# One packed load for the second norm's rows, and three modulation units summed on another engine

## The chip, the core and the metric

The kernel runs on one core of a Trainium2 chip. The metric is device time in microseconds for one execution, from the runtime's measurement; a profiled execution adds a trace, whose span runs from the first to the last instruction that the profiler recorded.

## What is computed

A transformer-like block on 512 tokens of width 1024, batch 1, all in float32. Cut to what matters here:

```
mod = silu(c) @ ada_w + ada_b                       # (1, 6144): six pieces of 1024
sh1, sc1, g1, sh2, sc2, g2 = split(mod, 6)
h = rmsnorm(x, norm1_g) * (1 + sc1) + sh1
xr, gr, u, v = split(h @ w_in, 4)                   # each 512 wide
y_lru = rg_lru(conv(xr)) * gelu(gr)                 # a scan over the sequence
y_sgu = gelu(u) * spatial_gating(gelu(v))
x = x + g1 * (concat(y_lru, y_sgu) @ w_out)
h = rmsnorm(x, norm2_g) * (1 + sc2) + sh2
x = x + g2 * moe(h)                                 # 32 experts, two per token
out = rmsnorm(x, final_g)
```

`ada_w` is 1024 x 6144 floats (25 MB), `w_in` 1024 x 2048, `w_out` 1024 x 1024, and each expert has three matrices of 2 MB, so the experts' 192 MB are most of what is read.

## The kernel before

**Modulation.** `ada_w` is cut into twelve units of 512 columns (`unit`, line 248 and on), each a 1024 x 512 matrix in two tiles of 1 MB, `self.w[0]` and `self.w[1]` (`Ada.load`). Units 0 to 3 feed the first norm, 4 and 5 the gate g1, 6 to 9 the second norm's shift and scale (6 and 8 the shift, 7 and 9 the scale), 10 and 11 the gate g2. `Ada.mm` (line 199) multiplies on TensorE: eight matmuls, one for each block `k` of 128 rows, with the column `cond[:, k]` spread over 32 columns as the stationary operand. Four of them lie side by side in the array, so that four partial sums come out on 32 rows each; ScalarE copies them to a `t2` tile (lines 209 and 211). `columns` (line 213) adds the four partial sums and turns 512 results into four columns, by matmuls with a matrix `quad` of ones at rows 0, 32, 64 and 96; `row` (line 220) does the same to a row on all partitions. `modulate2` (line 401) takes the columns of units 6 to 9 to `s2c`.

**Rows.** The second norm's gain `norm2_g` and the bias of its modulation (`ada_b[3072:5120]`) are wanted as columns in an order in which column `i` of a group holds every fourth element. Lines 257 to 264 load them with eight transfers of single floats, two rows or four rows each, into rows 40 to 63 of `rows_b`; one transpose (line 491) turns all of `rows_b`, and line 493 copies the 24 columns to `cols_g`.

**Order of the work.** SyncE issues nearly all loads, in program order, by hand throughout: an issue that waits for a free buffer holds all behind it. The 1 MB loads of `ada_w`, `w_in`, `w_out` and the first experts share five buffers (`w8`), given out in the order in which the earlier holders are done. Up to line 505 the order on every engine is written by hand; from there to line 830 a planner orders TensorE, VectorE, ScalarE and GpSimd from the program's order and its own estimate of costs and arrivals; then the order is by hand again to line 867. Each engine runs its list strictly in order.

The front: unit 0 and the first half of the `w_in` block for `xr` are loaded, then the rows of line 262, then units 1 and 2, the second half, unit 3 (lines 255 to 268). TensorE turns the normed `x` (line 383), multiplies unit 0, then runs `proj_step` (line 440) over the eight blocks of 128 rows, with units 1 to 3 between the steps: `unit[1].mm(0)` (line 476) after the first step, `unit[1].mm(1)` (line 478) in the midst of the second. Every float32 weight is split on the way into a high part (ScalarE, line 242) and a low part (VectorE, line 244), and a product takes three matmuls (high by high, low by high, high by low).

The middle: four projections (`v`, `gr`, `u` after `xr`), the recurrence, the gating (lines 657 to 671, for four blocks `c`), then the output projection in two halves: the first for all four token tiles, step by step (lines 709 to 722), the second tile by tile (lines 832 to 849), in which routing is worked in. `unit[8].mm` and `unit[9].mm` stand in the `u` projection (lines 649 and 650), `unit[10].mm` in the output projection (line 716), its `row` in the seventh step. `logit_bias` (line 732) works out the router's bias from the shift and scales the router's weights by the scale on GpSimd.

Then the experts, in blocks of two or four: SyncE streams their weights through a ring of buffers (line 1066), TensorE multiplies (lines 1119 and 1166).

Of the kernel before, what the change touches and what calls it, by code (L numbers as in the profile page):

```python
# [7 lines left out]
F32 = mybir.dt.float32  # L8
# [4 lines left out]
OP = mybir.AluOpType  # L13
AX = mybir.AxisListType

P = 128
# [29 lines left out]
def trunk(ctx, tc, a, out):  # L46
    nc = tc.nc
    sync, act, pool, dve, pe = nc.sync, nc.scalar, nc.gpsimd, nc.vector, nc.tensor
# [8 lines left out]
    fp = front.enter_context(tc.tile_pool(name="fp", bufs=1))  # L57
    mixer = ctx.enter_context(ExitStack())
    fa = mixer.enter_context(tc.tile_pool(name="fa", bufs=1, side="right"))
# [4 lines left out]
    def bank(tag=None, shape=(P, 512), dt=F32):  # L64
        if tag is None:
            tag = ring[turn[0] % 3]
            turn[0] += 1
        return psum.tile(list(shape), dt, name=tag)
# [10 lines left out]
    def t2(shape):  # L79
        return ft.tile(list(shape), F32, name="t2", bufs=6)  # L80
# [13 lines left out]
    def paired(v, n):  # L94

        return v.rearrange("p (k c i) -> p k i c", c=P, i=n)
# [9 lines left out]
    off = {}  # L106
# [15 lines left out]
    rows_b = fa.tile([P, P], F32, name="rows_b")  # L122
# [11 lines left out]
    ident = const.tile([P, P], F32, name="ident")  # L134
# [4 lines left out]
    dve.tensor_scalar(before, jp, 0.0, None, op0=OP.is_gt)  # L139
    ones = fp.tile([P, P], BF, name="ones")  # L140
    dve.memset(ones, 1.0)
    onesf = fa.tile([P, 64], F32, name="onesf")
    dve.memset(onesf, 1.0)
    pidx = fa.tile([P, P], F32, name="pidx")
# [20 lines left out]
    n = 0  # L165
# [3 lines left out]
    quad = fp.tile([P, P], F32, name="quad")  # L169
# [9 lines left out]
    class Ada:  # L179
# [18 lines left out]

        def mm(self, kk=None):
            if kk != 1:  # L200
                self.ps = bank("m")
            for k in range(KD) if kk is None else range(4 * kk, 4 * kk + 4):
                j = k % 4
                pe.matmul(self.ps[32 * j:32 * j + 32], cond[:, k:k + 1].to_broadcast([P, 32]), self.w[k // 4][:, j, :],  # L204
                          start=(k < 4), stop=(k >= 4), tile_position=(0, 32 * j))
            if kk != 0:
                self.m = t2((P, 512))
                if self.by4:
                    act.activation(paired(self.m, 1).rearrange("p k i c -> p (k i) c"), paired(self.ps, 4)[:, 0], AF.Copy)
                else:  # L210
                    act.activation(self.m, self.ps, AF.Copy)

        def columns(self):

            ps = bank("m", (P, 4))
            for q in range(4):
                pe.matmul(ps[:, q:q + 1], self.m[:, q * P:(q + 1) * P], quad[:, 0:1], start=True, stop=True)
            return ps

        def row(self, t):  # L220

            ps = bank("m")
            pe.matmul(ps, quad, self.m, start=True, stop=True)
            dve.tensor_tensor(t, ps, t, op=OP.add)

    class Block:
# [19 lines left out]
    unit = [Ada((256 * q, 1024 + 256 * q)) for q in range(4)]  # L246
# [7 lines left out]

    unit[0].load()
    b_xr.load(0)
    n = 40
    for name, ap in (("g2n", a["norm2_g"][0]), ("ada2", a["ada_b"][0, 3072:5120])):
        ap = ap.rearrange("(k c i) -> i k c", c=P, i=4)
        k = 4 * ap.shape[1]  # L260
        for i in range(4):
            sync.dma_start(rows_b[n + i:n + k:4], ap[i])  # L262
        off[name] = n - 40
        n += k
    unit[1].load()
    unit[2].load()
    b_xr.load(1)
# [42 lines left out]
    g2b = const.tile([P, D], F32, name="g2b")  # L310
# [26 lines left out]
    cond = fp.tile([P, KD], F32, name="cond")  # L337
    act.activation(cond, ident[:, 0:KD], AF.Silu)
    pt = bank("m", (P, KD))
# [13 lines left out]
    cols_g = fp.tile([P, 24], F32, name="cols_g")  # L353
# [4 lines left out]
    def cg(name, k):  # L358
        return cols_g[:, off[name] + k:off[name] + k + 4]
# [41 lines left out]
    def modulate2(u, q):  # L401

        ps = u.columns()
        n, sl = 4 * (q // 2), slice(4 * (q // 2), 4 * (q // 2) + 4)
        if q % 2 == 0:
            dve.tensor_tensor(s2c[:, 1, sl], ps, cg("ada2", n), op=OP.add)
            return
        t = small.tile([P, 4], F32, name="modt4")
        dve.scalar_tensor_tensor(t, ps, 1.0, cg("ada2", 8 + n), op0=OP.add, op1=OP.add)
        dve.tensor_tensor(s2c[:, 0, sl], t, cg("g2n", n), op=OP.mult)  # L410
# [24 lines left out]
    def split_to(n):  # L435
        while done[0] < min(n, len(flat)):
            high_to(done[0] + 1)
            low()

    def proj_step(b, k, ps, cs=range(4)):  # L440
        w, x = b.r[k], (hh[:, k, :], hl[:, k, :])
        for n, (i, j) in enumerate(((0, 0), (1, 0), (0, 1))):
            for c in cs:
                sl = slice(c * P, (c + 1) * P)
                lhs, rhs = (x[j][:, sl], w[i]) if b is b_v else (w[i][:, sl], x[j])
                pe.matmul(ps[c], lhs, rhs, start=(k == 0 and n == 0), stop=(k == KD - 1 and n == 2))  # L446

    def banks4():
        return [bank() for c in range(4)]
# [6 lines left out]
    pt = bank("m", (P, P))  # L456
# [17 lines left out]
    ps = banks4()  # L474
# [15 lines left out]
    pt = bank("m", (P, P))  # L490
    pe.transpose(pt, rows_b, ident)
    dve.tensor_copy(cols_b, pt)
    dve.tensor_copy(cols_g, pt[:, 40:64])
    sw = [t2((P, 4, P)) for i in range(2)]
    for i in range(2):
        act.dma_start(sw[i], a["sgu_w"][0].rearrange("h i j -> i h j")[:, 4 * i:4 * i + 4, :])
# [15 lines left out]
    for hp in range(2):  # L512
        pt = bank("m", (P, 4, P))
# [40 lines left out]
    for k in range(KD):  # L554
# [9 lines left out]
        if k == 4:  # L564
            pt = bank("m", (P, 4, P))
# [4 lines left out]
            for c in range(4):  # L570
                dve.scalar_tensor_tensor(sbb[:, c, :], pt[:, c, :], cb_("lnb", c), sbb[:, c, :], op0=OP.mult,
                                         op1=OP.add)
# [8 lines left out]
    for c in range(4):  # L581
        for i, t in enumerate((ra, ia)):
            ps = bank("m")
# [27 lines left out]
    ps = banks4()  # L611
# [31 lines left out]
    ps = banks4()  # L643
    for k in range(KD):
        proj_step(b_u, k, ps)
        if k % 2 == 1:
            split_to(29 + k)
        if k == 1:
            unit[8].mm()
            unit[9].mm()  # L650
        if k == 4:
            modulate2(unit[7], 1)
        if k == 6:
            modulate2(unit[8], 2)
    split_to(36)
    yy.append([l8(F32R), l8(F32R)])
    for c in range(4):
# [3 lines left out]
        for t in range(NT):  # L661
            for h in range(2):
                hd = 2 * c + h
                pe.matmul(sT[64 * h:64 * h + 64, t, :], vn[:, t, hd * 64:hd * 64 + 64], wT[:, hd, :],
                          start=True, stop=True, tile_position=(0, 64 * h))
# [3 lines left out]
                                 op0=OP.mult, op1=OP.add)  # L669
# [39 lines left out]
    ps = banks4()  # L709
    for k in range(KD):  # L710
        for t in range(NT):
            out_step(0, t, k, ps[t])
        if k % 2 == 1:
            split_to(37 + k)
        if k == 0:
            unit[10].mm()
        if k == 2:
            modulate2(unit[9], 3)
        if k == 5:
            unit[11].mm()  # L720
        if k == 6:
            unit[10].row(g2b[:, 0:512])
    split_to(44)
    for t in range(NT):
        out_add(0, t, ps[t])
# [4 lines left out]
        dve.tensor_copy(brep[kk], rep(sh2[:, 4 * kk:4 * kk + 4], P))  # L730

    def logit_bias():
        ps = bank("m", (P, 40))
        for k in range(KD):
            pe.matmul(ps, brep[k // 4][:, k % 4, :], wr[:, k, :], start=(k == 0), stop=(k == KD - 1))
        dve.tensor_tensor(rb, ps, rb, op=OP.add)
        for k in range(KD):
            pool.tensor_scalar(wr[:, k, :], wr[:, k, :], a2[:, k:k + 1], None, op0=OP.mult)
# [93 lines left out]
    for t in range(NT):  # L832
        ps = bank("h")
# [49 lines left out]
    ps = bank("m", (P, E))  # L883
# [412 lines left out]
    for b in range(NB):  # L1296
        q = b // 2
        n = min(2, NB - 2 * (q + 1))
# [14 lines left out]
        else:  # L1313
            n = max(0, len(fill) - FB - FA)
            comb = block(b, [], fill[:n], fill[n:n + FB], fill[n + FB:])
        if b == NB - 2:
            fg = xT4b[((NB - 1) // 2 + 1) % 2].rearrange("p (h k) s -> p h (k s)", h=2)[:, 0]
            for hf in range(2):
                gain = t2((P, 4, P))
                dve.tensor_copy(gain, rep(ca("fg", 4 * hf, 4), P))  # L1320
                ps = bank("m")
# [28 lines left out]
    ms, base, both, v, r = [fin[:, n_parts - 1 + i] for i in range(5)]  # L1350
# [70 lines left out]
```

## Time and profile before

| | |
|---|---|
| median of 3 runs | 723.99 us |
| lowest and highest | 723.14 and 724.71 us |
| the profiled execution: its own time | 725.12 us |
| the profiled execution: span | 723.3 us |
| TensorE busy | 658.3 us (91%) |
| VectorE busy | 297.0 us (41%) |
| ScalarE busy | 178.1 us (25%) |
| granted TensorE clock, mean | 0.962 of full |
| moved by DMA | 246.28 MB, 340 GB/s over the span |

In the rows, PE is TensorE's matmuls, PEld its weight loads, DVE is VectorE, ACT ScalarE, POOL GpSimd, SP SyncE; SPq is an issue of SyncE's DMA queue. Lnnn is a line of the kernel. `out<-in` gives tiles by their names in the program, without numbers; the tiles of the five load buffers are `w`, the PSUM banks are `m`, `h`, `y` and `c`. Times are microseconds from the span's start. A float32 matmul is two records in the trace, so one unit's eight matmuls are `x16`. The clock is the share of full speed that TensorE was granted: 0.50 is 1.2 GHz, 1.00 is 2.4 GHz.

### The profile page before, as it was taken

What the parts mean: (1) busy time and instruction counts of PE and PEld (TensorE: products, weight loads), DVE (VectorE), ACT (ScalarE), POOL (GpSimd) and SP (SyncE); (2) the same over time, 40 slices, a digit from 0 to 9 for tenths busy, and PEclk for the clock granted to TensorE, in tenths of its full rate; (3) what the DMA queues carried; (4) which work ended last, traced back from release to release, by engine and by line L of the source; (5) the groups of instructions that cost most, each with busy time, mean ns of one, the idle gap of its engine ahead of it and who ended that gap; (6) DMA issues with size and microseconds to landing.
All of it is one profiled execution on the core that took longest, in us unless ns stands there. A gap on an engine that the chain in (4) does not pass through costs nothing.

```text
span 723.3 us, 9703 instructions
## 1 busy us (share of the span) xinstructions
PE 658.3 (91%) x3693; PEld 358.2 (50%) x3693; DVE 297.0 (41%) x684; ACT 178.1 (25%) x317; POOL 25.0 (3%) x55
## 2 busy tenths in 40 slices
PE   7699999999998889987999999978799999998773
PEld 6356766777787444432444454513244445442132
DVE  7258638635468843321323333312132333224025
ACT  5135277532255121100101111000010111100114
POOL 3000001000103000000000000000000000000011
PEclk9799999999999999999999999989999999999887
DMA  8699902895528569999999999999999999999993
GB/s 295 200 346 305 318 24 97 271 367 183 218 124 316 218 255 427 400 422 420 421 423 420 420 419 422 420 421 419 423 421 420 420 422 420 421 421 421 383 335 120
DMA packets 68827, 246.28 MB, mean 340 GB/s; under 512 B 11064, under 2 KB 29096, under 8 KB 45224
## 3 DMA queue, kind: packets, MB, share of 16 engines
q1 hardware_dynamic: 67496, 245.08, 86.2%
q8 instruction: 30, 0.49, 0.3%
q10 hardware_dynamic: 1056, 0.52, 0.3%
q14 instruction: 21, 0.17, 0.1%
q0 software_dynamic: 224, 0.02, 0.0%
HBM read 243.51 MB, written 2.10 MB: 340 GB/s over the span
## 4 chain that ended last, share of the span: by engine, by line
PE 64%; DMA 21%; DVE 5%; ACT 4%; SPq 4%; issue 1%; POOL 0%; DVEq 0%; ACTq 0%
PE h L1119 21%; PE y L1166 11%; DMA w8r<-in_expert_w 10%; PE m L955 6%; DMA w<-in_expert_w 5%; PE c L969 4%; DMA l<-in_expert_w 4%; PE c L446 4%; PE h L446 3%; PE m L204 3%; PE y L446 2%; SPq L262 2%; DMA w<-in_ada_w 2%; SPq L1072 1%; PE h L90 1%
## 5 line engine op out<-in xcount | busy, mean ns | idle before, releaser
L1119 PE MATMUL h<-w,l 128*64 128x512 f32 (+1 forms) x616 | 152.5, 615 | 11.0 <-DMA w<-in_expert_w 11.0
L1119 PEld LDWEIGHTS h<-w,l 128*64 128x64 f32 (+1 forms) x616 | 42.8, 128 | 99.3 <-issue 76.6
L970 DVE TENSOR_TENSOR x<-x,c 128x512 f32<-128x512 f32 x96 | 65.8, 685 | 39.0 <-PE c L969 39.0
L1119 PE MATMUL h<-w8r,l 128*32 128x512 f32 (+1 forms) x304 | 69.8, 612 | 2.8 <-DMA w8r<-in_expert_w 2.8
L969 PE MATMUL c<-l,cT 128*128 128x512 f32 x192 | 62.6, 407 | 0.0
L1166 PE MATMUL y<-w8q,gT 128*64 128x512 f32 (+2 forms) x240 | 55.1, 626 | 5.2 <-DMA w8q<-in_expert_w 4.5
L1166 PE MATMUL y<-w8r,gT 128*64 128x512 f32 (+2 forms) x240 | 54.1, 611 | 5.5 <-DMA w8r<-in_expert_w 5.5
L955 PE MATMUL m<-l,b16h 128*128 128x256 f32 (+1 forms) x192 | 51.8, 294 | 3.1 <-ACT l L826 3.0
L994 DVE TENSOR_TENSOR t<-y,g2b 128x512 f32<-128x512 f32 x24 | 16.6, 691 | 92.3 <-PE y L1166 92.3
L1119 PE MATMUL h<-l,l 128*64 128x512 f32 (+1 forms) x120 | 52.5, 609 | 1.5 <-DMA l<-in_expert_w 1.5
L86 ACT ACTIVATE l<-t 128x512 fp32r<-128x512 f32 (+1 forms) x35 | 21.3, 612 | 128.5 <-DVE t L994 118.3
L1146 DVE SCALAR_TENSOR_TENSOR t<-t,ws,h 128x512 f32<-128x512 f32 x13 | 9.7, 747 | 97.2 <-PE h L1119 97.2
L955 PE MATMUL m<-l,b16l 128*128 128x256 f32 (+1 forms) x192 | 49.3, 281 | 0.0
L826 ACT ACTIVATE l<-m,s2c 128x256 f32<-128x256 f32 (+1 forms) x24 | 13.1, 546 | 146.2 <-PE m L955 146.2
L955 PEld LDWEIGHTS m<-l,b16h 128*128 128x128 f32 x192 | 36.3, 189 | 19.7 <-ACT l L826 8.3
L244 DVE TENSOR_TENSOR w8r<-w,w8r 128x512 fp32r<-128x512 f32 x48 | 30.6, 683 | 34.1 <-ACT w8r L242 34.1
L955 PEld LDWEIGHTS m<-l,b16l 128*128 128x128 f32 x192 | 36.3, 189 | 2.4
L1166 PEld LDWEIGHTS y<-w8r,gT 128*64 128x64 f32 (+1 forms) x240 | 15.4, 132 | 42.2 <-issue 30.0
L446 PE MATMUL c<-b16h,w8r 128*128 128x512 f32 x80 | 32.3, 427 | 4.2 <-ACT b16h L415 3.7
L242 ACT ACTIVATE w8r<-w 128x512 fp32r<-128x512 f32 x48 | 26.9, 621 | 33.1 <-PE h L92 14.1
L1119 PEld LDWEIGHTS h<-w8r,l 128*32 128x32 f32 (+1 forms) x304 | 17.8, 123 | 34.3 <-issue 28.9
L969 PEld LDWEIGHTS c<-l,cT 128*128 128x128 f32 x192 | 29.4, 189 | 6.7 <-DVE x L970 4.2
(359 smaller groups left out, 941.3 us busy)
## 6 DMA issues: line engine op xcount, KB each, us to landing
w<-in_expert_w SPq DMA_DIRECT2D x77, 1024.0 KB
w8r<-in_expert_w SPq DMA_DIRECT2D x60, 1024.0 KB
w8q<-in_expert_w SPq DMA_DIRECT2D x30, 1024.0 KB
l<-in_expert_w SPq DMA_DIRECT2D x17, 1024.0 KB
w<-in_ada_w SPq DMA_DIRECT2D x16, 1024.0 KB
w<-in_ada_w SPq DMA_DIRECT2D x16, 512.0 KB
w<-in_w_in SPq DMA_DIRECT2D x8, 1024.0 KB
w<-in_w_out SPq DMA_DIRECT2D x4, 1024.0 KB
```

The costliest lines, as they stand in the source:

```text
L86: act.activation(hi, src, AF.Copy)
L204: pe.matmul(self.ps[32 * j:32 * j + 32], cond[:, k:k + 1].to_broadcast([P, 32]), self.w[k // 4][:, j, :], start=(k < 4), stop=(k >= 4), ti ...
L242: act.activation(hi, raw, AF.Copy)
L244: return lambda: dve.tensor_tensor(lo, raw, hi.bitcast(F32), op=OP.subtract)
L262: sync.dma_start(rows_b[n + i:n + k:4], ap[i])
L446: pe.matmul(ps[c], lhs, rhs, start=(k == 0 and n == 0), stop=(k == KD - 1 and n == 2))
L955: pe.matmul(hold[k], src[:, t, chunk(k)], g[:, t, :], start=(t == 0 and i == 0), stop=(t == NT - 1 and i == 1))
L969: pe.matmul(ps, cT[:, t, :], y[:, cs], start=(i == 0), stop=(i == 1))
L970: dve.tensor_tensor(x2[:, t, cs], x2[:, t, cs], ps, op=OP.add)
L994: dve.tensor_tensor(yf, y, g2b[:, cs], op=OP.mult)
L1119: pe.matmul(h[c:c + n], xT[:, k, c:c + n], w[j][k], start=(k == 0), stop=(k == KD - 1), tile_position=(0, c))
L1166: pe.matmul(y[c:c + n], gT[:, q, c:c + n], w, start=(q == 0), stop=(q == FC - 1), tile_position=(0, c))
```

## The change

The second norm's rows are loaded into a tile of their own, `rows_d`, as six rows of 512 contiguous floats, in two transfers (two rows and four rows) at the same place in SyncE's queue. Four transposes with a step of four elements bring them into the same 24 columns of `cols_g`.

Units 8, 9 and 10 have a new method, `add`, in place of `mm`: for each block `k`, VectorE multiplies the 128 x 512 block of weights by the column `cond[:, k]` and adds it to a `t2` tile, in place. The tile then holds a partial sum on every partition, and `columns` and `row` use a column of ones, `one`, in place of `quad`. The tile keeps the weights' order of columns, so `columns` reads it with a step of four. Unit 8's sums stand in the steps of the `u` projection, those of units 9 and 10 in the steps of the output projection's first half; unit 8's columns move from step 6 of the `u` projection to step 1 of the output projection, unit 9's from step 2 to behind the loop, unit 10's row into `logit_bias`.

```diff
@@ -139,6 +139,8 @@
     dve.tensor_scalar(before, jp, 0.0, None, op0=OP.is_gt)
     ones = fp.tile([P, P], BF, name="ones")
     dve.memset(ones, 1.0)
+    one = fp.tile([P, 1], F32, name="one")
+    dve.memset(one, 1.0)
     onesf = fa.tile([P, 64], F32, name="onesf")
     dve.memset(onesf, 1.0)
     pidx = fa.tile([P, P], F32, name="pidx")
@@ -198,7 +200,7 @@
 
         def mm(self, kk=None):
             if kk != 1:
-                self.ps = bank("m")
+                self.ps, self.sum = bank("m"), quad
             for k in range(KD) if kk is None else range(4 * kk, 4 * kk + 4):
                 j = k % 4
                 pe.matmul(self.ps[32 * j:32 * j + 32], cond[:, k:k + 1].to_broadcast([P, 32]), self.w[k // 4][:, j, :],
@@ -210,17 +212,29 @@
                 else:
                     act.activation(self.m, self.ps, AF.Copy)
 
+        def add(self, k):
+
+            w = self.w[k // 4][:, k % 4, :]
+            if k == 0:
+                self.m, self.sum = t2((P, 512)), one
+                dve.tensor_scalar(self.m, w, cond[:, 0:1], None, op0=OP.mult)
+            else:
+                dve.scalar_tensor_tensor(self.m, w, cond[:, k:k + 1], self.m, op0=OP.mult, op1=OP.add)
+
         def columns(self):
 
             ps = bank("m", (P, 4))
             for q in range(4):
-                pe.matmul(ps[:, q:q + 1], self.m[:, q * P:(q + 1) * P], quad[:, 0:1], start=True, stop=True)
+                m = self.m[:, q * P:(q + 1) * P]
+                if self.sum is one and self.by4:
+                    m = paired(self.m, 4)[:, 0, q]
+                pe.matmul(ps[:, q:q + 1], m, self.sum[:, 0:1], start=True, stop=True)
             return ps
 
         def row(self, t):
 
             ps = bank("m")
-            pe.matmul(ps, quad, self.m, start=True, stop=True)
+            pe.matmul(ps, self.sum[:, 0:1].to_broadcast([P, P]) if self.sum is one else quad, self.m, start=True, stop=True)
             dve.tensor_tensor(t, ps, t, op=OP.add)
 
     class Block:
@@ -254,14 +268,10 @@
 
     unit[0].load()
     b_xr.load(0)
-    n = 40
-    for name, ap in (("g2n", a["norm2_g"][0]), ("ada2", a["ada_b"][0, 3072:5120])):
-        ap = ap.rearrange("(k c i) -> i k c", c=P, i=4)
-        k = 4 * ap.shape[1]
-        for i in range(4):
-            sync.dma_start(rows_b[n + i:n + k:4], ap[i])
-        off[name] = n - 40
-        n += k
+    rows_d = fa.tile([6, 512], F32, name="rows_d")
+    sync.dma_start(rows_d[0:2], a["norm2_g"][0].rearrange("(k f) -> k f", f=512))
+    sync.dma_start(rows_d[2:6], a["ada_b"][0, 3072:5120].rearrange("(k f) -> k f", f=512))
+    off["g2n"], off["ada2"] = 0, 8
     unit[1].load()
     unit[2].load()
     b_xr.load(1)
@@ -490,7 +500,10 @@
     pt = bank("m", (P, P))
     pe.transpose(pt, rows_b, ident)
     dve.tensor_copy(cols_b, pt)
-    dve.tensor_copy(cols_g, pt[:, 40:64])
+    pt = bank("m", (P, 4, 6))
+    for i in range(4):
+        pe.transpose(pt[:, i, :], rows_d.rearrange("r (c i) -> r i c", i=4)[:, i, :], ident[0:6, 0:6])
+    dve.tensor_copy(cols_g.rearrange("p (r i) -> p i r", i=4), pt)
     sw = [t2((P, 4, P)) for i in range(2)]
     for i in range(2):
         act.dma_start(sw[i], a["sgu_w"][0].rearrange("h i j -> i h j")[:, 4 * i:4 * i + 4, :])
@@ -645,13 +658,9 @@
         proj_step(b_u, k, ps)
         if k % 2 == 1:
             split_to(29 + k)
-        if k == 1:
-            unit[8].mm()
-            unit[9].mm()
+        unit[8].add(k)
         if k == 4:
             modulate2(unit[7], 1)
-        if k == 6:
-            modulate2(unit[8], 2)
     split_to(36)
     yy.append([l8(F32R), l8(F32R)])
     for c in range(4):
@@ -712,14 +721,13 @@
             out_step(0, t, k, ps[t])
         if k % 2 == 1:
             split_to(37 + k)
-        if k == 0:
-            unit[10].mm()
-        if k == 2:
-            modulate2(unit[9], 3)
+        unit[9].add(k)
+        unit[10].add(k)
+        if k == 1:
+            modulate2(unit[8], 2)
         if k == 5:
             unit[11].mm()
-        if k == 6:
-            unit[10].row(g2b[:, 0:512])
+    modulate2(unit[9], 3)
     split_to(44)
     for t in range(NT):
         out_add(0, t, ps[t])
@@ -730,6 +738,7 @@
         dve.tensor_copy(brep[kk], rep(sh2[:, 4 * kk:4 * kk + 4], P))
 
     def logit_bias():
+        unit[10].row(g2b[:, 0:512])
         ps = bank("m", (P, 40))
         for k in range(KD):
             pe.matmul(ps, brep[k // 4][:, k % 4, :], wr[:, k, :], start=(k == 0), stop=(k == KD - 1))
```

## Rows read from the trace of the kernel before

**Rows 1.** The profile page: the chain that ended last, by engine.

```profile
PE 64%; DMA 21%; DVE 5%; ACT 4%; SPq 4%; issue 1%; POOL 0%; DVEq 0%; ACTq 0%
```

**Rows 2.** From 270 us: TensorE's wait (total, times, longest); two windows, GB/s last.

```profile
PE h L1119 <- DMA w<-in_expert_w: 11.0, 8, 2.3
...
262.00:271.00 9.00, 8.29 (x42) 3.51 (x44) 0.76 (x2) 0.60 (x1) 0.00 (x0) 1.00 0.26 83
271.00:290.00 19.00, 18.82 (x98) 8.80 (x96) 7.03 (x13) 3.02 (x5) 0.00 (x0) 1.00 1.01 424
```

**Rows 3.** SyncE's queue, 0 to 60 us: start, duration, issue (x: how many merged).

```profile
9.51 10.19 SPq L262 DMA_DIRECT2D rows_b<-in_norm_g  x4
19.73 4.06 SPq L262 DMA_DIRECT2D rows_b<-in_ada_b  x4
23.84 9.21 SPq L194 DMA_DIRECT2D w<-in_ada_w  x8
```

**Rows 4.** Windows of the front: length, busy PE PEld DVE ACT POOL, clock, DMA share, GB/s.

```profile
16.00:17.00 1.00, 0.55 (x8) 0.00 (x0) 0.00 (x0) 0.38 (x1) 0.00 (x0) 1.00 0.95 346
17.00:18.00 1.00, 0.73 (x7) 0.73 (x7) 0.00 (x0) 0.70 (x2) 0.00 (x0) 1.00 0.35 54
...
24.00:25.00 1.00, 1.00 (x4) 0.81 (x3) 0.00 (x0) 0.00 (x0) 0.00 (x0) 0.50 0.28 2
...
26.00:27.00 1.00, 0.19 (x1) 0.00 (x0) 0.00 (x0) 0.00 (x0) 0.00 (x0) 0.87 0.96 314
...
30.00:31.00 1.00, 1.00 (x8) 0.00 (x0) 0.00 (x0) 0.00 (x0) 0.00 (x0) 0.50 1.00 343
```

**Rows 5.** Timeline of the front: ScalarE and TensorE, with idle time before and its releaser.

```profile
18.80 1.15 ACT L242 ACTIVATE w8r<-w 128x512 fp32r<-128x512 f32 x2 [1.09 <-DMA w<-in_w_in]
...
25.56 0.63 PE L446 MATMUL c<-b16l,w8r 128*128 128x512 f32 x1
29.65 1.94 PE L204 MATMUL m<-w,cond 128*32 128x512 f32 x8 [3.46 <-DMA w<-in_ada_w]
...
34.34 1.06 PE L204 MATMUL m<-w,cond 128*32 128x512 f32 x8 [0.46 <-DMA w<-in_ada_w]
35.33 0.50 PE L446 MATMUL y<-b16h,w8r 128*128 128x512 f32 x1
...
36.83 0.95 PE L217 MATMUL m<-quad,t 128*128 128x1 f32 x8
...
41.54 2.78 PE L204 MATMUL m<-w,cond 128*32 128x512 f32 x16
```

**Rows 6.** What TensorE waited for, 36 to 118 us (first) and 118 to 190 (second).

```profile
PE c L446 <- DVE w8r L244: 0.5, 1, 0.5
...
PE m L204 <- DMA w<-in_ada_w: 1.0, 1, 1.0
```

**Rows 7.** Timeline of TensorE: unit 8's matmuls and the next one.

```profile
135.86 1.92 PE L204 MATMUL m<-w,cond 128*32 128x512 f32 x16
137.71 0.50 PE L446 MATMUL c<-b16h,w8r 128*128 128x512 f32 x1
```

**Rows 8.** Windows of the middle, columns as in rows 4.

```profile
150.00:158.00 8.00, 8.00 (x51) 5.46 (x44) 0.48 (x3) 0.66 (x2) 0.00 (x0) 1.00 1.05 387
158.00:170.00 12.00, 11.98 (x105) 8.09 (x104) 10.04 (x16) 7.17 (x13) 0.00 (x0) 1.00 0.50 169
170.00:182.00 12.00, 12.00 (x58) 10.06 (x57) 2.83 (x6) 2.31 (x4) 0.00 (x0) 1.00 0.70 264
```

**Rows 9.** The convolution's lines 548 and 550: duration in ns, least, median, most.

```profile
L548 DVE TENSOR_SCALAR l<-l,cols_b x4: 537/538/546, 66.2 to 74.2; 128x512 f32<-128x512 f32 x4
...
L550 DVE SCALAR_TENSOR_TENSOR l<-l,cols_b,l x12: 739/742/750, 67.2 to 77.9; 128x511 f32<-128x511 f32 x4, 128x510 f32<-128x510 f32 x4, 128x509 f32<-128x509 f32 x4
```

**Rows 10.** SyncE's issue of w_out's last blocks; the output projection's second half, first matmul.

```profile
166.88 1.23 SPq L234 DMA_DIRECT2D w<-in_w_out  x2
...
190.74 0.39 PE L90 MATMUL h<-w8r,l 128*128 128x512 f32 x1
```

## Prediction

> **What bounds the kernel now.** I read the page's chain of waits first [rows 1]. TensorE holds 64% of the chain, DMA 21%. The DMA part lies late: from 270 us on TensorE waits 11.0 us for one kind of the experts' buffers alone, while before 271 the transfers wait for TensorE: between 262 and 271 us they moved 83 GB/s, then 424 [rows 2]. So the expert stream is full from 271 us to near the end, its length is fixed by its bytes, and it starts when TensorE frees buffers. Whatever brings TensorE to 271 us sooner brings the end sooner by as much.
>
> Then the front. SyncE's queue needs from 9.5 to 23.8 us to issue the eight small transfers of line 262, and only behind them stands unit 1's load [rows 3]. The windows show what this does: the transfer engines move 346 GB/s until 17, and from 18 to 25 next to nothing (2 GB/s), with about a quarter of the engines' time still busy [rows 4]. TensorE's list answers: the first projection's last matmul starts at 25.56; unit 1's halves start at 29.65 and 34.34, both when their data lands [rows 5]. That is a stall on the chain.
>
> Last the stretch 118 to 190 us: TensorE waited there 1.0 us in all, so it is the bound [rows 6], and three modulation units of 1.85 us each [rows 7] are what the change takes away. VectorE beside it is idle for long: 0.48 busy of 8 us in 150 to 158, 10.04 of 12 in 158 to 170, 2.83 of 12 in 170 to 182 [rows 8].
>
> **Front: the rows.** Removed are eight transfers in 4-byte elements (24 x 128 of them); added are two with 2 KB rows, at the same place in the queue. Two issues, even at the 1.0 us of each of the later four (4.06 for 4), end by 11.5, so unit 1's load follows there instead of at 23.84 [rows 3]. The stream then does not dry up at 17.5; unit 1's 2.1 MB at 346 GB/s take 6.1 us, so they land by about 24 to 25. The projection ends at 25.56 + 0.43 = 26.0. Unit 1's first half is there, and what is late next is TensorE itself.
>
> How fast it goes from there depends on its clock. The granted clock was 0.50 from 20 to 25, 0.87 in 26 to 27 (so it rose to 2.4 GHz about 0.26 us into that stretch, after five microseconds of matmuls), stayed 1.00 while the engine idled, and was back at 0.50 (1.2 GHz) in 30 to 31 [rows 4]. I take it that without the idle stretch it stays up: the half unit costs 0.26 us slow and 0.86 x 0.99 = 0.85 fast (0.99 is 34.34 to 35.33), together 1.1; the six matmuls behind it 1.5 (35.33 to 36.83) [rows 5]. The second half starts at 26.0 + 1.1 + 1.5 = 28.6 instead of 34.34: 5.7 us gained. If the clock fell anyway, the half costs the 1.9 of the one at 29.65 and the six 6 x 0.43 = 2.6 (0.43 is 512 columns at 1.2 GHz): start at 30.5, 3.8 gained. The Trainium skill, "TensorE: Matmul & The Clock Gate", Part 1, holds that the slow clock is the default, that activity lifts it and idleness brings it back; by that the sum is the first one, and this trace agrees, since the clock came up after the matmuls and fell after the wait.
>
> One cost: the first block of w_in, which line 242 awaits at 18.80 [rows 5], has unit 1's stream behind it now. Between 17 and 18 only 0.35 of the engines' time was busy [rows 4]; if the late engines had to share with full ones it would land at most 0.65 us later, at least 0. I take 0.3, near the middle. The front's gain is 5.4, between 3.2 and 5.7.
>
> The rest of this edit is nothing. Four more transposes of six rows stand ahead of the fifth projection step: about 4 x 0.12 us, by the eight one-column matmuls of line 217 in 0.95 [rows 5]. TensorE waits there 0.5 us for a split of VectorE anyway [rows 6]; if that cover is gone, 0.5 us. The copy of the 24 columns and the memset are one short VectorE instruction each.
>
> **Middle: units 8, 9 and 10.** TensorE loses three times eight packed matmuls; one unit holds it 135.86 to 137.71 = 1.85 us [rows 7], three 5.6, or 5.8 by the 1.92 that the row itself gives. ScalarE loses three copies. The column sums and unit 10's row remain, the row moved in front of the router bias: same TensorE time, and its VectorE addition falls where VectorE waits for that bias.
>
> Added on VectorE: per unit one scaling and seven multiply-adds, each reading its predecessor's result. The nearest rows are the causal convolution's, the same two forms over the same width, in place: 0.54 + 7 x 0.74 = 5.7 us a unit [rows 9], 17.2 in all. Unit 8's fall into the idle time before 158. Units 9 and 10 have 11.4 us to find, and 7.5 us idle in 150 to 158, 2.0 in 158 to 170 and 9.2 in 170 to 182 [rows 8]. If unit 9's go early and all of unit 10's land among the spatial-gating work, that work ends 5.7 - 2.0 = 3.7 us later, and at worst the output projection waits as long; at best nothing waits. I take 0.2, near nothing, since the later projection steps that need those results are the fifth and on: four steps of twelve matmuls, some 3 us each by the six in 1.5, lie between.
>
> What stands behind these instructions: VectorE's queue is in order, and behind a sum that waits for its weights stand the low halves of w_out's splits and the gating products, for which TensorE waits. And the sums free the load buffers later than the matmuls did, which holds SyncE's queue: unit 8's frees the second block of w_out, unit 10's now frees w_out's last two blocks (issued 166.88) and the first expert loads. Those blocks are first multiplied at 190.74 [rows 10], over 20 us later, so this costs nothing until unit 10 is some 15 us late.
>
> The middle's gain: 5.6 - 0.2 = 5.4, between 5.6 - 3.7 = 1.9 and 5.8.
>
> **Sum.** 5.4 + 5.4 = 10.8. The profiled execution took 725.12 us, 1.8 beyond its span; it becomes 714.3. It lies 1.1 above the median of the runs, 723.99, which becomes 713.2. Bounds: least gain 3.2 + 1.9 = 5.1, 718.9. Most: 5.7 + 5.8, plus 0.9 if the slow stretch at 41.54 (a whole unit in 2.78 instead of 1.85, [rows 5, 7]) doesn't come back, plus the 1.0 of waiting in the middle [rows 6]: 13.4, 710.6.
>
> **Rivals.**
> - *Front only.* VectorE's sums delay gating or splits by as much as TensorE saves. For it: VectorE is 10.04 of 12 us full where the gating runs. Against: the idle stretches on both sides. 723.99 - 5.4 = 718.6. Chance 0.12.
> - *Middle only.* Unit 1 would not come sooner, because the new transfers, too, take long or the queue was full anyway. For it: one issue of line 262 sat until the stream had passed. Against: from 18 to 25 there was no stream to be full of. 723.99 - 5.4 = 718.6. Chance 0.05.
> - *Neither*: both of these, or the gain lost on the way to 271 us. 724. Chance 0.04.
> - *Slower.* Unit 10's sums come last in VectorE's queue, its buffers come free late, SyncE's queue holds w_out's last blocks, and TensorE stands before the second half of the output projection. It decides from the point where unit 10's first half is freed after about 185 us of the old time (190.74 [rows 10], less some 5 for a block: 3.0 to load 1 MB at 346 GB/s [rows 4], 1.15 for a split [rows 5], and an issue), and each further microsecond costs one; to pass 725.4 it must eat 10.8 + 1.4 = 12.2, so free it at 197. VectorE's work up to 182 plus 11.4 fits long before. 727 for a release near 199. Chance 0.04.
>
> **How the numbers follow.** The forecast, both gains within their bounds, has 0.75: 713.2. The range 710.6 to 718.7 takes in the bounds of both and the one-sided rivals at 718.6, and leaves out some 0.1. About 0.2% (1.4 us) is what a measurement of this kernel can tell from no change. Faster by more: 0.75 + 0.12 + 0.05 = 0.92; within: 0.04; slower: 0.04.
>
> **What would show it.** Right: line 262 gone, unit 1's load issued near 10, the stream above 300 GB/s through 17 to 25, line 204's third and fourth half units near 26.0 and 28.6 with the clock up; the output projection's second half starting near 180 instead of 190.7; the expert stream full from about 260. Wrong in the front: a wait for unit 1 still there, or the clock down between 27 and 31. Wrong in the middle: TensorE waiting for VectorE (splits, gating or a sum) between 118 and 190, by more than the 1.0 of before. Wrong as a whole: both stages shorter but the expert stream not starting sooner.

## The result, and the profile after

The changed kernel takes **713.85 us** (median of 4 runs, 712.62 to 714.13) where the kernel before, run beside it, takes 724.35 (723.14 to 725.71): a ratio of 0.9848, 95% interval 0.9827 to 0.9868. The profiled execution took 712.62 us with a span of 710.8, 12.5 less than before, at a mean granted clock of 0.983 against 0.962.

The front first. SyncE's queue from 9 to 30 us (start, duration, issue), which answers to [rows 3]:

```profile
10.43 1.15 SPq L272 DMA_DIRECT2D rows_d<-in_norm_g  x1
11.62 0.27 SPq L273 DMA_DIRECT2D rows_d<-in_ada_b  x1
11.94 12.31 SPq L196 DMA_DIRECT2D w<-in_ada_w  x8
```

Unit 1's load now follows at 11.94 instead of 23.84. The windows of the changed kernel (length, busy PE PEld DVE ACT POOL, clock, DMA share, GB/s; [rows 4] before) show that the stream no longer dries up:

```profile
17.00:18.00 1.00, 0.29 (x5) 0.01 (x1) 0.00 (x0) 0.66 (x2) 0.00 (x0) 1.00 1.08 365
...
20.00:21.00 1.00, 0.26 (x1) 0.26 (x2) 1.00 (x3) 1.00 (x2) 0.00 (x0) 1.00 1.11 356
...
24.00:25.00 1.00, 1.00 (x4) 0.63 (x2) 0.00 (x0) 0.00 (x0) 0.00 (x0) 0.50 1.10 347
25.00:26.00 1.00, 1.00 (x10) 0.16 (x8) 0.00 (x0) 0.00 (x0) 0.00 (x0) 0.94 1.10 346
...
30.00:31.00 1.00, 1.00 (x10) 0.92 (x8) 0.83 (x2) 0.66 (x2) 0.00 (x0) 1.00 1.06 382
```

From 24 to 25 us 347 GB/s were moved where it had been 2, and from 26 to 31 TensorE is busy throughout at a granted clock of 1.00 (2.4 GHz). Its timeline over the same stretch ([rows 5] before):

```profile
24.82 0.54 PE L456 MATMUL c<-b16l,w8r 128*128 128x512 f32 x1
25.29 1.07 PE L206 MATMUL m<-w,cond 128*32 128x512 f32 x8
...
27.89 1.06 PE L206 MATMUL m<-w,cond 128*32 128x512 f32 x8
...
34.60 1.92 PE L206 MATMUL m<-w,cond 128*32 128x512 f32 x16
```

Both halves of unit 1 run without a wait, the second at 27.89 instead of 34.34. Unit 2 starts 6.9 us sooner (34.60 for 41.54) and takes 1.92 instead of 2.78, so in this execution the slow stretch there is gone.

In the middle, first the waits of TensorE from 112 to 190 us (total, times, longest; [rows 6] before). Then the weight loads of the column sums in line 231 (LDWEIGHTS; duration in ns: least, median, most; first and last start), with `quad` and with `one`. Then one group of column sums on the timeline:

```profile
PE m L206 <- DMA w<-in_ada_w: 0.9, 1, 0.9
PE m L744 <- DVE t L738: 0.4, 1, 0.4
```

```profile
L231 PEld LDWEIGHTS m<-quad,t x48: 186/192/192, 18.0 to 136.4; 128*128 128x128 f32 x48
...
L231 PEld LDWEIGHTS m<-one,t x16: 308/329/332, 154.5 to 176.7; 128*128 128x128 f32 x16
```

```profile
175.31 1.80 PE L231 MATMUL m<-one,t 128*128 128x1 f32 x8
```

Here is something that was not in the forecast. The column sums of units 8 and 9, which now read their weights in place with a step of four floats, take 1.80 us a group where the others take 0.95 [rows 5], because each weight load takes 329 ns instead of 192. There is also a new wait of 0.4 us ahead of the router bias.

VectorE in the same kernel (the sums are lines 220 and 222; in square brackets the idle time before, and what ended it):

```profile
131.44 3.90 DVE L222 SCALAR_TENSOR_TENSOR t<-w,cond,t 128x512 f32<-128x512 f32 x5
...
159.69 6.71 DVE L222 SCALAR_TENSOR_TENSOR t<-w,cond,t 128x512 f32<-128x512 f32 x10
173.47 0.69 DVE L697 TENSOR_TENSOR t<-h,g1b 128x512 f32<-128x512 f32 x1 [7.07 <-PE h L92]
```

After the last sum VectorE idles 7.07 us, so the sums have room. SyncE's last loads of `w_out`, which unit 10's buffers could have held up, go out from 161.13 on, against 166.88 [rows 10]:

```profile
161.13 5.01 SPq L248 DMA_DIRECT2D w<-in_w_out  x2
```

Counted from the first scan, which is itself 8.1 us sooner, that is 2.3 us later, but TensorE does not wait for them. The output projection's second half starts at 176.97, where the forecast said near 180.

At the end, two windows 12 us earlier than those of [rows 2], and from the list of TensorE's waits, from 258 us on, the one shown there:

```profile
250.00:259.00 9.00, 7.95 (x42) 4.04 (x44) 0.65 (x2) 0.60 (x1) 0.00 (x0) 1.00 0.28 88
259.00:278.00 19.00, 18.80 (x98) 9.26 (x96) 7.14 (x13) 3.02 (x5) 0.00 (x0) 1.00 1.01 423
```

```profile
PE h L1128 <- DMA w<-in_expert_w: 11.9, 9, 1.5
```

The expert stream is full from 259 instead of 271 and as full as before (423 GB/s for 424); what the earlier stages save arrives at the end.

Four landmarks of TensorE and VectorE make the ledger: the first scan of the recurrence, the first matmul of the router bias, the first expert matmul, and the span's end (723.3 before, 710.8 after). Before:

```profile
120.27 1.21 DVE L608 TENSOR_TENSOR_SCAN l<-l,l 128x512 f32<-128x512 f32 x1
...
195.69 1.87 PE L735 MATMUL m<-wr,t 128*128 128x40 f32 x16
...
242.41 7.51 PE L1119 MATMUL h<-w,l 128*64 128x512 f32 x33
```

After:

```profile
112.19 1.22 DVE L621 TENSOR_TENSOR_SCAN l<-l,l 128x512 f32<-128x512 f32 x1
...
183.99 1.95 PE L744 MATMUL m<-wr,t 128*128 128x40 f32 x16 [0.45 <-DVE t L738]
...
230.41 7.51 PE L1128 MATMUL h<-w,l 128*64 128x512 f32 x33
```

So the part up to the scans is 8.1 us shorter, scans to bias 3.6 (75.4 to 71.8), bias to experts 0.3, experts 0.5.

### The profile page after: what moved, and what is told of

The parts are those of the page before. It is cut to its first block, busy times and chain, and to the rows that moved or that the text cites. A ratio compares the mean times of both kernels' runs of the same rounds, so it can differ in the third digit from the quotient of the medians.

```text
span 710.8 us, 9636 instructions
## 1 busy us (share of the span) xinstructions
PE 644.6 (91%) x3649; PEld 358.5 (50%) x3649; DVE 312.3 (44%) x709; ACT 176.3 (25%) x314; POOL 25.0 (4%) x55
## 4 chain that ended last, share of the span: by engine, by line
PE 33%; DMA 28%; SPq 1%; DVE 1%; ACT 1%; issue 0%; ACTq 0%
PE h L1128 15%; DMA w<-in_expert_w 11%; DMA w8r<-in_expert_w 10%; PE y L1175 8%; DMA l<-in_expert_w 7%; PE m L964 4%; PE c L978 4%; SPq L1081 1%; PE m L1143 1%; PE m L986 1%; ACT l L835 0%; PE m L992 0%; DVE x L1370 0%; DVE x L1391 0%; ACT x L1390 0%
## 5 line engine op out<-in xcount | busy, mean ns | idle before, releaser
L1128 PE MATMUL h<-w,l 128*64 128x512 f32 (+1 forms) x616 | 148.4, 601 | 12.0 <-DMA w<-in_expert_w 11.9
L1128 PE MATMUL h<-w8r,l 128*32 128x512 f32 (+1 forms) x304 | 70.9, 607 | 4.3 <-DMA w8r<-in_expert_w 4.3
L1175 PE MATMUL y<-w8r,gT 128*64 128x512 f32 (+2 forms) x240 | 51.7, 590 | 7.4 <-DMA w8r<-in_expert_w 7.4
L1175 PE MATMUL y<-w8q,gT 128*64 128x512 f32 (+2 forms) x240 | 52.2, 592 | 5.5 <-DMA w8q<-in_expert_w 4.5
L1128 PE MATMUL h<-l,l 128*64 128x512 f32 (+1 forms) x120 | 50.8, 593 | 1.6 <-DMA l<-in_expert_w 1.6
L456 PE MATMUL c<-b16h,w8r 128*128 128x512 f32 x80 | 30.8, 411 | 3.0 <-ACT b16h L425 3.0
L1146 DVE SCALAR_TENSOR_TENSOR ws<-m,of 128x4 f32<-128x4 f32 (+1 forms) x13 | 2.1, 163 | 70.4 <-PE m L1143 70.4
```

The lines of the kernel that those rows point to most:

```text
L1128: pe.matmul(h[c:c + n], xT[:, k, c:c + n], w[j][k], start=(k == 0), stop=(k == KD - 1), tile_position=(0, c))
L1175: pe.matmul(y[c:c + n], gT[:, q, c:c + n], w, start=(q == 0), stop=(q == FC - 1), tile_position=(0, c))
```

## The experiments

No kernel here leaves out part of the computation; one adds matmuls whose result nobody reads. Each time is a median of several runs, beside runs of the kernel before in the same series (723.59, 723.82 and 723.64 us in the three series). The intervals are 95% intervals of the ratio to the kernel before.

### The two halves alone

Edits: the kernel before with the hunks on `rows_d` and its four transposes only (first), and with the hunks on `one`, `Ada.add`, `columns`, `row` and their calls only (second).

> The kernel before with the two packed row transfers alone. Theory (the two edits gain separately, the rows 8.1 us by the traces of before and after at 105 us): unit 1's second half on TensorE near 28, clock up at unit 2's matmuls, 8.1 us less than before, some 716. Rival (unit 1's wait gives only the 5.4 us of the forecast, the rest comes from the units): some 718.5.

> The kernel before with the three units' sums on VectorE alone; the eight transfers in single floats stay. Theory (the units gain 4.0 us by the traces): some 720, TensorE's front as before. Rival (the sums fit only because the front had drawn everything ahead): no gain, 724. Rival (they gain the 5.4 forecast): 718.6.

Rows only: **719.51 us**, ratio 0.9941 (0.9924 to 0.9959), 4.1 us gained. Units only: **720.08 us**, 0.9949 (0.9931 to 0.9967), 3.5 gained. By the landmarks the halves lie where they should: scans to bias take 75.3 us with the rows alone, as before, and 71.8 with the units alone, as after. So 3.6 us is what the units' edit is worth there. The rows' gain is less sharp: 4.1 us by the medians, 6.7 by the first scan of the two profiles (113.6 for 120.3). TensorE's timeline of the rows-only kernel shows one reason:

```profile
27.79 1.06 PE L204 MATMUL m<-w,cond 128*32 128x512 f32 x8
...
34.74 3.30 PE L204 MATMUL m<-w,cond 128*32 128x512 f32 x16
```

Unit 1's second half is where the changed kernel has it (27.89), but unit 2 ran at the slow clock, 3.30 us for 1.92. Which matmuls of the front meet the slow clock differs between executions, so one profiled pair cannot give the front's gain to a microsecond.

### Is it the transfers' form or their place?

The kernel before with its eight transfers of single floats, only moved behind unit 3's load (their transpose moved later too); and the changed kernel with the two transfers cut into eight, of 512 bytes a row:

```
     b_xr.load(0)
+    unit[1].load()
+    unit[2].load()
+    b_xr.load(1)
+    unit[3].load()
     n = 40
...
-    unit[1].load()
-    unit[2].load()
-    b_xr.load(1)
-    unit[3].load()
...
```

> The kernel before with its eight transfers in single floats moved behind unit 3's load, and the transpose that needs them behind unit 3's columns. Theory (they hurt only by what stands behind them in SyncE's queue): units 1 to 3 come early, and the transfers fall where the queue has time to spare; most of the 8.1 us kept, 716 to 718. Rival (3072 transfers of 4 bytes slow whatever runs beside or behind them, wherever they stand): the next loads, the v projection's, come late instead, 720 to 724.

```
...
+    for q in range(4):
+        cq = slice(128 * q, 128 * q + 128)
+        sync.dma_start(rows_d[0:2, cq], a["norm2_g"][0].rearrange("(k f) -> k f", f=512)[:, cq])
...
```

> The changed kernel with its two row transfers cut into eight, of 512 contiguous bytes a row. Theory (the elements cost, not the number of issues): each issue some 0.3 to 1 us, unit 1's load issued by 16 at the latest, before the stream runs dry at 17.5; as the changed kernel, 713.8. Rival (eight issues are enough to hold the queue): unit 1 issued near 20 or later, up to 5 us slower.

Moved: **718.15 us**, 0.9926 (0.9901 to 0.995), 5.7 gained, no less than the rows edit. SyncE's queue in that kernel:

```profile
10.49 14.55 SPq L194 DMA_DIRECT2D w<-in_ada_w  x8
...
33.33 7.50 SPq L266 DMA_DIRECT2D rows_b<-in_norm_g  x4
40.87 6.06 SPq L266 DMA_DIRECT2D rows_b<-in_ada_b  x4
```

The single floats hold the queue 13.6 us here (7.50 + 6.06), about as long as in [rows 3], but nothing urgent stands behind them. The price was the place in the queue. Eight issues: **715.18 us**, 0.9879 (0.9844 to 0.9914); its queue, and TensorE's second half of unit 1:

```profile
13.17 5.91 SPq L277 DMA_DIRECT2D rows_d<-in_ada_b  x4
19.12 8.91 SPq L196 DMA_DIRECT2D w<-in_ada_w  x8
```

```profile
29.35 1.06 PE L206 MATMUL m<-w,cond 128*32 128x512 f32 x8 [1.46 <-DMA w<-in_ada_w]
```

Eight issues of longer runs still hold unit 1's load until 19.12, and TensorE waits 1.46 us. Expected was 16 at the latest, and near 20 by the rival, so the issue time is closer to the rival's. The wait is the right size for the 1 us or so by which it is slower than the changed kernel's 713.85 and 714.30 of other series, though the intervals overlap.

### Is the front's gain the clock?

The kernel before with twenty short matmuls put where TensorE waits for unit 1:

```
+    keep_warm(20)
     unit[1].mm(0)
```

> The kernel before with twenty more warming matmuls on TensorE while it waits for unit 1; their result is used nowhere. Theory (the wait also cost clock, which accounts for the part of the front beyond the forecast): the clock stays up, unit 1's second half still starts at 34.3 on its data, but unit 2's matmuls take 1.85 instead of 2.78 us and all behind comes some 1.3 us sooner, 723. Rival (the slow stretch at 40 to 43 us comes from the short waits at 38 to 39): still there, 724.3.

**724.54 us**, ratio 1.0022 (1.0001 to 1.0042). Windows of this kernel, columns as above:

```profile
27.00:28.00 1.00, 1.00 (x11) 1.00 (x11) 0.00 (x0) 0.00 (x0) 0.00 (x0) 1.00 1.08 380
...
30.00:31.00 1.00, 0.94 (x8) 0.19 (x8) 0.00 (x0) 0.00 (x0) 0.00 (x0) 1.00 1.09 363
```

The clock is 1.00 in 30 to 31, where it was 0.50 before [rows 4], and by the medians no time is gained. Unit 2 and the first scan in the same trace:

```profile
40.10 1.92 PE L204 MATMUL m<-w,cond 128*32 128x512 f32 x16
```

```profile
117.60 1.21 DVE L609 TENSOR_TENSOR_SCAN l<-l,l 128x512 f32<-128x512 f32 x1
```

Unit 2 runs fast, as the theory had it and the rival had not, and the first scan and the first expert matmul (239.7) stand 2.7 us sooner than in the profile before. But the experts' stretch took 482.8 us in this execution, for 480.9, and the median is the rival's. The two profiles of the units alone, which have the old front, put the first scan at 118.1 and 119.3, within 2 us of this one; every kernel here with unit 1's load ahead of the small transfers, or behind two packed ones, has it between 111.9 and 114.3. So the front's gain is mainly the data that comes sooner; a gain from the clock alone is not shown by the runs.

### The column sums in order

The changed kernel, with all eight adds of units 8 and 9 writing their sum in the order in which the columns are read, so that the column sums load contiguous weights; and the same with unit 11 on VectorE too:

```
...
+            if self.by4:
+                w = w.rearrange("p (c i) -> p c i", i=4)
+                m = m.rearrange("p (i c) -> p c i", c=P)
...
-            if self.sum is one and self.by4:
-                m = paired(self.m, 4)[:, 0, q]
...
```

> The changed kernel, with VectorE writing units 8 and 9 in the order of the columns, so that the column matmuls read their weights without a step. Theory (the stepped weight load, 329 instead of 192 ns, is what the middle lost): each group of column sums back from 1.66 to about 0.8 us, 1.7 us less than the changed kernel, some 712. Rivals: the sums on VectorE become as much slower by the stepped writing (the same time on the chain if they stay hidden, more if not); or the wait before the router bias takes up what is saved, 713.8.

```
-        if k == 5:
-            unit[11].mm()
+        unit[11].add(k)
```

> The kernel of the run before this one, with unit 11 summed on VectorE as well. Theory (TensorE bounds the output projection, VectorE is idle from 166 to 173 us): 2.0 us less again, some 710. Rival (VectorE is full by then: the sums delay the low halves of w_out's second half and the residual additions): no gain or some us more, 712 to 716.

In order: **711.81 us**, 0.9824 (0.98 to 0.9849). With unit 11 as well: **715.67 us**, 0.989 (0.9847 to 0.9934). The records of the adds (line 227) and of the weight loads (line 234) in the first of them:

```profile
L227 DVE SCALAR_TENSOR_TENSOR t<-w,cond,t x21: 739/1147/1203, 131.3 to 170.9; 128x512 f32<-128x512 f32 x21
```

```profile
L234 PEld LDWEIGHTS m<-one,t x16: 187/192/192, 156.9 to 177.5; 128*128 128x128 f32 x16
```

TensorE's loads are back at 192 ns, but VectorE's adds now pay: 1147 ns in the median where the plain ones take some 750. Of the 1.7 us saved, only 0.6 is seen from scans to bias (71.2 for 71.8), because TensorE now waits 0.7 us for a low half of `w_out`. With unit 11 on VectorE too, that wait (TensorE's waits from 112 to 232 us) becomes

```profile
PE h L92 <- DVE w8r L261: 3.4, 2, 3.1
```

and the stretch from the scans to the experts grows from 117.7 to 122.4 us, so VectorE is the bound there: with the adds of units 8 and 9 as slow as these a fourth unit doesn't fit beside the three. A fourth unit beside plain adds was not run.

### Only the last sum in order, and the parts side by side

Once more the changed kernel and its two halves, in one series, and the changed kernel with only the eighth add of units 8 and 9 in order:

```
...
+                if self.by4 and k == KD - 1:
+                    self.m = t2((P, 512))
+                    out = self.m.rearrange("p (i c) -> p c i", c=P)
+                    m = m.rearrange("p (c i) -> p c i", i=4)
+                    w = w.rearrange("p (c i) -> p c i", i=4)
+                dve.scalar_tensor_tensor(out, w, cond[:, k:k + 1], m, op0=OP.mult, op1=OP.add)
...
```

> The changed kernel as it is, beside its two halves in the same call. If the two halves add, it is faster than before by the sum of e9 and e10. The theory (the halves lie in different stretches and each passes its whole gain on to the end) expects 713 to 714.5 us, 9.5 to 11 us under before; with e9 and e10 at 4 to 5 us each the sum would be 8 to 9.5. The rival (the rows edit alone passes less on, because something later waits anyway until the units edit takes it out of the way) expects that the sum of e9 and e10 falls short of this gain by 1.5 us or more, and that the stretch from the scans to the first expert matmul is longer in e9 than in the kernel before.

> The kernel before with the rows edit alone, once more. The theory (front gain 5 to 8 us, by how fast unit 2's matmuls run on TensorE in this execution) expects 716 to 719 us, and from the scans to the first expert matmul 122 us as in the kernel before. Unit 1's second half near 27.9 us on the span in either case; unit 2's sixteen matmuls at 1.9 or at 3.3 us tell how much of the gain the clock took.

> The kernel before with the units edit alone, once more. The theory (4.0 us, three units' matmuls out less 1.7 us for the column sums from stepped weights) expects 719 to 720 us, and 118 us from the scans to the first expert matmul. The forecast's own size of this half, 5.4 us, would give 718.5 and 116.7 us there.

> The changed kernel with one edit: only the eighth add of units 8 and 9 writes its result in the order in which the column sums read it, into a tile of its own; the seven before it stay as they were. The theory (the stepped weight load of the column sums costs 1.7 us on TensorE, and writing all eight adds out of order cost VectorE that much again in e3) expects column sums of 0.95 us a group, one VectorE add a unit of 1.1 to 1.2 us in place of 0.7, no new wait of TensorE on VectorE over 0.5 us, and a time 1 to 1.7 us under e8. The rival (TensorE's time there is not on the path; the 4.0 us of the units edit are short for another reason) expects the same time as e8 within 0.5 us, and 118.2 us from the scans to the first expert matmul as in the changed kernel.

| kernel | median us | ratio (95% interval) | gained us | scans to bias us |
|---|---|---|---|---|
| changed, again | 714.30 | 0.987 (0.9847 to 0.9893) | 9.3 | 71.8 |
| rows only, again | 718.26 | 0.9924 (0.9901 to 0.9948) | 5.4 | 75.3 |
| units only, again | 720.81 | 0.9956 (0.9941 to 0.9972) | 2.8 | 71.9 |
| last sum in order | 712.18 | 0.9849 (0.9824 to 0.9874) | 11.5 | 70.9 |

**The halves add.** 5.4 + 2.8 = 8.2 against 9.3, which is inside the interval of the latter (7.7 to 11.1). The shortfall of 1.1 us is under the 1.5 that the rival named, but by the spread of the runs it is uncertain by nearly 2 us, so the times alone don't decide it. The traces do: from the scans to the first expert matmul the rows-only kernel takes 122.0 us, where the kernel before takes 122.1, so nothing there swallows its gain.

**The front's size.** One pair of profiles with unit 2 fast in both. Units only, again:

```profile
34.69 1.06 PE L206 MATMUL m<-w,cond 128*32 128x512 f32 x8
...
41.40 1.92 PE L206 MATMUL m<-w,cond 128*32 128x512 f32 x16
```

Changed, again:

```profile
25.90 1.21 PE L206 MATMUL m<-w,cond 128*32 128x512 f32 x8
28.63 1.06 PE L206 MATMUL m<-w,cond 128*32 128x512 f32 x8
...
35.35 1.92 PE L206 MATMUL m<-w,cond 128*32 128x512 f32 x16
```

That is 6.06 us at the second half and 6.05 at unit 2. In this execution of the changed kernel the clock had been down through the end of the first projection, and the halves stand at 25.90 and 28.63. No pair is exact, though: the units-only kernel of the first series had unit 2 just as fast, at 40.16, only 4.8 us behind this one. Averaged, the first scan stands at 113.0 in the seven profiles with the two packed transfers and at 119.2 in the three with the old front (the one with the added matmuls left out). That makes 6.2 us, with single pairs between 3.7 and 8.3.

**The last sum in order** is the fastest version by median but for the one with all sums in order (711.81, in another series; the two are not told apart). Its adds (line 228), its column sums' loads (line 235) and its waits from 112 to 190 us:

```profile
L228 DVE SCALAR_TENSOR_TENSOR t<-w,cond,t x21: 742/746/1151, 129.2 to 166.0; 128x512 f32<-128x512 f32 x21
```

```profile
L235 PEld LDWEIGHTS m<-one,t x16: 188/192/193, 154.8 to 175.4; 128*128 128x128 f32 x16
```

```profile
PE m L206 <- DMA w<-in_ada_w: 0.8, 1, 0.8
PE h L92 <- DVE w8r L262: 0.7, 1, 0.7
PE m L748 <- DMA w<-in_expert_w: 0.5, 1, 0.5
```

Only one add a unit pays the 1.15 us, and the loads are fast. Scans to bias give 0.9 of the 1.7 us, since 0.7 goes into a wait for a split of `w_out` that the changed kernel doesn't show, a little over the 0.5 us allowed for. Another 1.1 us is gained between bias and experts (45.5 us for 46.6), where a wait of 2.3 us in the routing was 0.8 in this execution. The kernel with the single floats moved, which changes nothing there, has the same wait at 0.8, so it is not the work of the last sum; what shortened it is not settled. Against the changed kernel of the same series the mean of five runs is 1.7 us lower, 95% interval -0.3 to 3.7 by the spread of the runs, so the times alone don't settle that it is faster. Against the kernel before it is.

## Why the prediction was right, and where it was off

**The time.** 713.2 was forecast; 713.85 and 714.30 were measured. The 10.8 us of gain are 10.5 and 9.3. That the first of them is so close is in part luck: the middle came out 1.5 to 1.9 us short, and in the traces the front came out larger by about half of that. The range's upper end, 718.7, is 0.2 below the 718.9 that the prediction's own least gain gives; nothing hung on it.

**The chain.** That whatever brings TensorE to the experts sooner brings the end sooner by as much held: 12.0 us sooner at the first expert matmul and 12.5 at the end of the profiled pair. The stretch of the experts itself ran 479.5 to 482.8 us in the profiles taken here, so a single pair is no finer than that: with the added matmuls TensorE reached the experts 2.7 us sooner and the span ended only 0.8 sooner.

**The front.** Each step came as put: the two issues end by 11.9 (11.5 forecast), unit 1 is there when the projection ends, TensorE is what is late next. The halves were forecast at 26.0 and 28.6 and stood at 25.90 and 28.63 in one profile; in the other the first projection ended sooner, since the clock was still at 1.00 in 20 to 21 instead of 0.50. Without the idle stretch the clock is 1.00 from 26 to 31. The Trainium skill, "TensorE: Matmul & The Clock Gate", Part 1, named in the prediction, holds that activity lifts the slow clock; the trace agrees there. It did not stay up in every execution: in three of the seven other profiles in which TensorE does not wait for unit 1, unit 2 took 2.14, 3.30 and 3.47 us instead of 1.92. The 0.3 us for a later block of `w_in` was not there: ScalarE starts on it at 18.84 against 18.80 [rows 5].

```profile
18.84 1.15 ACT L256 ACTIVATE w8r<-w 128x512 fp32r<-128x512 f32 x2 [0.41 <-DMA w<-in_w_in]
```

The four transposes took 0.64 us, with no wait behind them. The front's term, 5.4, is 4.1 and 5.4 by the medians of the rows alone and 6.2 by the averaged traces. The 8.1 of the first pair lies near the top of what such pairs give; 0.9 of it is the slow unit 2 of the profile before (the prediction had kept that for its upper bound) and 0.7 the earlier end of the first projection after.

**The middle.** This term was mis-sized: 5.4 forecast, 3.4 to 3.6 from scans to bias in each pair of profiles (3.9 to the experts in the first), and 3.5 and 2.8 by the medians of the units alone. The 5.6 us of matmuls went, and VectorE's sums cost what was said (0.48 + 7 x 0.75 = 5.7 us a unit) and fitted into its idle time without delaying gating or splits. The step that failed is "The column sums and unit 10's row remain ... same TensorE time". They remained, but in the kernel before ScalarE's copy out of PSUM had put units 6 to 9 in order on the way, at no more than a plain copy (line 209 reorders, line 211 doesn't):

```profile
L209 ACT ACTIVATE t<-m x4: 572/597/598, 121.0 to 155.9; 128x512 f32<-128x512 f32 x4
```

```profile
L211 ACT ACTIVATE t<-m x8: 597/597/598, 16.6 to 184.4; 128x512 f32<-128x512 f32 x8
```

With the copy gone the column sums read a step of four floats, and their loads take 329 ns: 2 x (1.80 - 0.95) = 1.7 us. Another 0.4 us is a wait before the router bias. Ahead of the copies that it waits for, VectorE now does unit 9's two short scale instructions and four splits in a row, where two splits stood there before (1.28 us at 193.78):

```profile
180.90 2.50 DVE L258 TENSOR_TENSOR w8r<-w,w8r 128x512 fp32r<-128x512 f32 x4
```

Which of these makes the wait, no run separates. 5.6 - 1.7 - 0.4 = 3.5. The Trainium skill, "SBUF — State Buffer", Door 1, says that consecutive accesses within one line of 16 bytes are at full bandwidth and that each crossing to a new line pays. With a step of four floats each access is on a new line, and the loads of 329 ns, 192 once the data lies in order, agree; the page gives no price. The prediction had not asked what a stepped load costs.

**The rivals.** *Front only* fell: VectorE's sums delay nothing by as much as TensorE saves. *Middle only* and *neither* fell with the timeline of the front. *Slower* needed unit 10's buffers to come free after 185 us to cost anything; the loads behind them went out from 161.13 on. The mechanism of the first rival, VectorE holding up TensorE, shows in the run with a fourth unit.

## What to carry to other kernels

Ask of each small transfer what stands behind it in its queue: here its place cost about 5 us, and its form nothing measurable once it stood behind the urgent loads. When a reduction moves to another engine, look at what the removed copy did on the way (order, layout), since the next reader pays for it; reorder in the last step only, where one pass of VectorE pays and not eight (the times of the two versions, 712.18 and 711.81 us, do not tell them apart; VectorE's room does). And before moving a further piece of work to an idle engine, count the idle time that is left: beside three units, two of them with the slow adds, a fourth cost 3.9 us.

## What the runs showed of the hardware

- A 128 x 128 float32 weight load from elements 16 bytes apart took 329 ns, from contiguous ones 192.
- A VectorE multiply-add over 512 floats took 1151 ns with only its result written in steps of 512 bytes, 1147 with the running sum read and written so, and 746 plain. ScalarE's copy out of PSUM that reorders by reading every fourth element took 597 ns, as the plain one.
- Which stretch of the front meets the slow clock differs between executions of one kernel (unit 2 in 1.92, 2.14, 2.42, 2.78, 3.30 or 3.47 us in the profiles taken here), which moves the end of the front by a microsecond or two.
